# Half-block products for the forgetting heads' gates, and weight sums by adding transfers

## The chip, the cores and the metric

The kernel runs on one core of one Trainium2 chip, in one launch. The metric is the device time of an execution in microseconds (us), as the median of several runs. TensorE (PE) multiplies into PSUM; VectorE (DVE) and ScalarE (ACT) do elementwise work; GpSimd (POOL) and SyncE (SP) here mostly issue transfers, which run on the core's sixteen DMA engines. SP's transfers appear as queue q1 of the profile, POOL's as q0. Only POOL's transfers can add into what already lies at their destination.

## The reference

A decoder layer with two groups of eight heads: latent attention (MLA) and forgetting attention (FoX). Both groups have a gate path. The parts that this document needs:

```python
h = _rms_norm(x, g_pre)                     # x: 512 tokens x 2048, float32
proj = h @ w_in
(q_lat, kv_lat, k_rope_raw, gate_mla,
 fq, fk, fv, f_logit, gate_fox) = jnp.split(proj, split_points, axis=-1)
...
log_f = jax.nn.log_sigmoid(f_logit + b_forget)
c = jnp.cumsum(log_f, axis=1)               # per forgetting head
logits = q @ k * scale + c_query - c_key    # causal softmax, times v
...
o_fox = _fox_branch(fq, fk, fv, f_logit, b_forget) * jax.nn.silu(gate_fox)
o = jnp.concatenate([o_mla, o_fox], axis=-1) @ w_out
return x + _rms_norm(o, g_post)
```

`fv` and `gate_fox` are each a product of 512 x 2048 with 2048 x 1024. All arithmetic is float32.

## The kernel before

**Matrix products.** A float32 product is made from two parts of each operand: `hi`, a cast by Scalar (line 279 for weights), and `lo`, the remainder, subtracted by Vector (line 282). Three matmuls (lines 150 to 152) add hi x hi, hi x lo and lo x hi. Normalised x, without its row factor, lies on chip as `hh` and `hl`, sixteen tiles of 128 features x 512 tokens; the row factor is applied to the results (`rcol` by token as a column, `rrow` as a row).

**Chunks.** All weights pass as a list of chunks of at most 128 x 1024 numbers (512 KB). `load` lets SP bring a chunk to a `raw` tile four chunks ahead, `divide` splits it two chunks ahead of its matmuls. A chunk that is a sum of two blocks can be loaded as `raw` and `second` and joined by Vector (line 269).

**Two forms of a projection.** `proj_T` (used by `fox_q`, `fox_k`, `fox_g`) takes weights as the stationary operand and all 512 tokens as the moving one: 16 k-tiles x 2 heads x 3 matmuls of 512 columns for two heads. `product` makes one of the seven half-block products of a Strassen-Winograd scheme: x is cut into two halves of tokens and two halves of features, the weights into two halves of rows and two of columns, and p1, p2, p4, q6, g7, g5 and g3 replace eight half-size products. Each takes eight k-tiles in four chunks. With `turned=False` tokens end up on partitions, 48 matmuls of 512 columns a product; with `turned=True` features end up on partitions, 96 matmuls of 256 columns. Before the change the values of the forgetting heads ("v"), the latents ("l", turned) and the MLA gates ("m") are made like this; the gates of the forgetting heads are made by `fox_g`, two heads at a time, in four passes.

**Sums of x blocks.** `x_steps` puts x together again, `away_steps` makes the sums and sends them to DRAM, `fetches` bring them back and `divisions` split them.

**Sums of weight blocks.** `sum_blocks` lists background steps `bg`: SP copies one block to a DRAM tile (line 324), POOL adds the second (line 320). `paced` advances them by a step each `pace` k-tiles, twice that for the double-size steps of the output projection. A tiny mark written from the current weight tile (line 326) holds a step's copy to its place. The pace starts at 4; `set_pace` sets 20 after the first gates, 8 before the first queries, 12 before product q6 and 4.9 for the heads.

**Order.** After the first projection (`proj_first`, in which the order on Vector, Scalar and TensorE is fixed by hand) come: gates 0, p1, gates 1, p2, gates 2, g5, queries 0, g3, keys 0, q6, p4, g7, then the head pairs, with queries and keys of the next pair around the attention of the last; gates 3 come after the last keys. Elsewhere a planner orders each engine's instructions and may draw work forward. Small tasks in `todo` are taken one at a time after a k-tile (`pump`), or all at once (`drain`): the forget sums `fs` (17 steps on eight rows of 512), the rotary tables `rot`, the sums of x.

The values, scaled by `rcol`, are sent to DRAM (`v_out`) and brought back for each pair of heads. The finished gates wait on chip in `gf` tiles.

Of the kernel before, what the change touches and what calls it, by code (L numbers as in the profile page):

```python
# [66 lines left out]
def tile_hybrid_layer(  # L67
# [69 lines left out]
    def split_into(hi, lo, src, scale=None, pin=False):  # L137
        if scale is None:
            a = act.copy(hi, src)
            b = dve.tensor_tensor(out=lo, in0=src, in1=hi.bitcast(F32), op=ALU.subtract)  # L140
            if pin:
                in_order(a, b)
        else:
            act.mul(hi, src, scale)
            dve.scalar_tensor_tensor(
                out=lo, in0=src, scalar=scale, in1=hi.bitcast(F32), op0=ALU.mult, op1=ALU.subtract
            )

# [70 lines left out]
    raws, ready, up_chunks, early = {}, {}, set(), set()  # L219

    more, deep, seconds = [], [], [vr, 2]
    needs = {}

    def raw_tile(i):
# [4 lines left out]
        if i <= prods["g7", "v"][-1] and i % 5 < 2:  # L229
            return vr.tile([P, 1024], F32, tag="raw", name=f"raw{i}", bufs=2)  # L230
# [3 lines left out]
    def load(i, small=None):  # L234

        w, cols, k, n, width = chunks[i]
        assert state["step"] >= needs.get(i, -3) + 2
        if cols is None:
# [5 lines left out]
            if k is not None:  # L244
                if seconds and i not in early:
                    pool, bufs = seconds
                    second = pool.tile([P, 2, 512], F32, tag="second", name=f"second{i}", bufs=bufs)
# [24 lines left out]
    def divide(i):  # L272
# [10 lines left out]
        ready[i] = [t[:, :m].rearrange("p (k c) -> p k c", k=n) for t in (hi, lo)]  # L283

# [80 lines left out]
    AT = {"v": O_FV, "l": 0, "m": O_GM}  # L365
# [6 lines left out]
    for g in "vlm":  # L372
# [17 lines left out]
    for n in ("g0", "p1", "g1", "p2", "g2", "s5", "q0", "s3", "k0", "s6", "p4", "s7",  # L390
              "q1", "k1", "q2", "k2", "q3", "k3", "g3"):
        name = {"p1": "p1", "p2": "p2", "p4": "p4", "s5": "g5", "s3": "g3", "s6": "q6", "s7": "g7"}.get(n)
        if name:
            add_products([(name, "v")], plain_in)
            if n == "s5":
                early.update(prods["g5", "v"][2:])
        else:
            at = {"q": O_FQ, "k": O_FK, "g": O_GF}[n[0]] + 256 * (3 - int(n[1]))
            fox[int(n[1])][n[0]] = add_chunks(w_in, [(0, at, 256)], NK, 4, 256)
    add_products(  # L400
        [
            ("p1", "l"), ("p1", "m"), ("p2", "l"), ("p4", "l"), ("p2", "m"), ("p4", "m"),
# [188 lines left out]
    def proj_first(rng, banks):  # L591

        squares = deque(range(2 * NK))
# [232 lines left out]
    def rotary_tables():  # L826
        ifc = cst.tile([P, 2], F32, name="ifc")
        nc.sync.dma_start(ifc, inv_freq)
        pi = vr.tile([P, S], I32, tag="c", name="pos")
# [4 lines left out]
        def names():  # L834
            nonlocal n1, n2
            nn = vr.tile([P, 2, S], F32, tag="c", name="nn")
# [231 lines left out]
    def fox_q(p):  # L1068

        qb = [proj_bank(f"fq{p}{i}") for i in range(2)]  # L1070
        proj_T(fox[p]["q"], [(qb[i], P, two[i]) for i in range(2)], hh, hl)
        q = []
        wholes = slot(f"fw{p}")
        for i in range(2):
            t = tmp(f"fqt{p}{i}")
            dve.scalar_tensor_tensor(out=t, in0=qb[i], scalar=SC_F, in1=rrow, op0=ALU.mult, op1=ALU.mult)
            q.append(split(t, f"fq{p}{i}", first=P))
            whole_block(wholes, i, t)
# [26 lines left out]
    def values_into(tiles, cols, parts, pin=False):  # L1105
        for t in range(NT - 1):
            hi, lo = tiles[t]
            split_into(hi[:, cols], lo[:, cols], parts[t], pin=pin)
        last = act.copy(tiles[NT - 1][:, cols], parts[NT - 1])
        if pin:  # L1110
            in_order(last)
# [35 lines left out]
    hcol, ncol, rneg = (cst.tile([P, NT], F32, name=n) for n in ("hcol", "ncol", "rneg"))  # L1147
# [20 lines left out]
    def split_v(pair, both):  # L1168

        tiles = v_pair(f"fv{pair}")  # L1170
        return lambda: values_into(tiles, slice(0, 256), [both[:, t, :] for t in range(NT)], True)

    gates, gate_slots = {}, {}

    def fox_g(p, gb):

        proj_T(fox[p]["g"], [(gb[i], P, two[i]) for i in range(2)], hh, hl)
        if p == 3:
            drain()
        both = gate_slots[p] = slot(f"gf{p}")  # L1180
        for i in range(2):
            h = 2 * (3 - p) + i
            gates[h] = gate_of(gb[i], both[:, i, :], f"f{h}")
# [3 lines left out]
    def v_block(name):  # L1187
        return vr.tile([P, 2, S], F32, tag="c", name=name)
# [16 lines left out]
    act.mul(rneg, rcol, -1.0)  # L1205
# [11 lines left out]
    fox_g(0, [att_bank("fg00"), bank("pv", "fg01", 1)])  # L1217
    drain()
    set_pace(20)
    rot = rotary_tables()  # L1220
    wait(1)
    todo.extend([*fs[13:], *rot[:3]])
    A = two_of(proj_bank, "va")
    product("p1", "v", x_block(0, 0), A, True, True)
    drain()
    pa, pb = v_block("vpa"), v_block("vpb")
    scaled_copy(pa, A, 0, rcol)
    scaled_copy(pb, A, 2, rcol)
    todo.extend([*x_steps(0), *x_steps(1)])
    fox_g(1, two_of(proj_bank, "fg1"))  # L1230
    drain()
    todo.extend(rot[3:10])
    product("p2", "v", x_block(1, 0), A, False, True)
    drain()
    c11 = v_block("vc11")
    scaled_copy(c11, A, 0, rcol)
    v_out(c11, 0, 0)
    todo.extend([*x_steps(2), *x_steps(3)])
    fox_g(2, two_of(proj_bank, "fg2"))
    drain()  # L1240
    f3, f6, f7 = (fetches(n, "m") for n in ("g3", "q6", "g7"))
    d3, d6, d7 = (divisions(n, "m") for n in ("g3", "q6", "g7"))
    G = two_of(att_bank, "vg")
    product("g5", "v", operand("g5", "m"), G, True, True)
    c22 = v_block("vc22")
    scaled(c22, G, 2, pb, ALU.subtract, rcol)
    todo.extend([*f3, *rot[10:14], *d3, *rot[14:]])
    set_pace(8)
    q, wholes = fox_q(0)
    drain()  # L1250
    product("g3", "v", operand("g3", "m"), G, False, True)
    c12 = v_block("vc12")
    scaled(c12, G, 0, pa, ALU.subtract, rcol)
    todo.extend([*f6, *[lambda: None] * 3, *d6])
    k = fox_k(0, wholes)
    drain()
    set_pace(12)
    C = two_of(proj_bank, "vc")
    product("q6", "v", operand("q6", "m"), C, True, True)
    scaled(c12, C, 0, c12, col=rcol)  # L1260
    v_out(c12, 0, 1)
    todo.extend([*f7, *d7[:2]])
    B = two_of(proj_bank, "vp4")
    product("p4", "v", x_block(1, 2), B, True, True)
    drain()
    c21 = v_block("vc21")
    scaled(c21, B, 2, pb, col=rcol)
    product("g7", "v", operand("g7", "m"), C, False, True, side=d7[2:])
    c22, c22_sum = slot("vo22"), c22
    scaled(c22, C, 2, c22_sum, col=rcol)  # L1270
    v_out(c22, 1, 1)
    c21, c21_sum = slot("vo21"), c21
    scaled(c21, C, 2, c21_sum, col=rneg)
# [605 lines left out]
```

## Time and profile before

| what | us |
|---|---|
| median of 3 runs | 893.63 |
| lowest and highest run | 893.61, 893.68 |
| the profiled execution: span from first to last instruction | 892.3 |
| TensorE busy in it | 880.3 |
| VectorE, ScalarE, GpSimd busy | 660.2, 462.1, 72.8 |

The profile is of one execution, and gives its time as the span; the median is 1.3 us above that. Busy time of TensorE is a union of overlapping matmuls; the durations of single ones include the pipeline, so rates are read from starts. The DMA share is the mean busy share of the sixteen engines, summed over their queues. Values' and gates' products, first queries and first keys lie between 41.7 and 231 us, the pairs of forgetting heads between 231 and 418 us.

### The profile page before, as it was taken

The page shows a single profiled execution, that of the slowest core. Times are in us where ns is not written, and L with a number is a line of the kernel's source. Part 1 is how long each engine was busy: PE and PEld are TensorE (multiplying, and loading weights), DVE is VectorE, ACT ScalarE, POOL GpSimd, SP SyncE. Part 2 cuts the span into 40 slices and gives each one's busy share as a digit, 9 for nine tenths or more (in the row PEclk, how much of TensorE's full clock was granted, in tenths as well). Part 3 has the DMA queues.
Part 4 walks back from the last instruction along what each step waited for, and adds up shares of the span by engine and source line. Part 5 has one row for each costly group of instructions (what it writes and reads, how often), then busy time and mean ns, then how long its engine had stood idle before and what let it go on. Part 6 is the DMA issues. An engine that isn't in the chain of part 4 may idle for free.

```text
span 892.3 us, 12700 instructions
## 1 busy us (share of the span) xinstructions
PE 880.3 (99%) x4486; PEld 748.2 (84%) x4486; DVE 660.2 (74%) x1106; ACT 462.1 (52%) x841; POOL 72.8 (8%) x92
## 2 busy tenths in 40 slices
PE   9999999999999999999999999999999999999996
PEld 9988887888888888888998999788888888888885
DVE  4579995648665546477678999979787895988786
ACT  6944434334343433335455565657465776646383
POOL 0110110011110211010000000000000000000021
PEclk9999999999999999999999999999999999999999
DMA  9998798889999999997799885697988637799878
GB/s 319 277 265 241 212 341 279 250 214 315 261 282 275 238 230 225 247 231 186 243 412 410 329 303 178 167 275 166 221 182 215 153 111 233 228 323 322 264 214 254
DMA packets 139235, 225.07 MB, mean 252 GB/s; under 512 B 16898, under 2 KB 68892, under 8 KB 138148
## 3 DMA queue, kind: packets, MB, share of 16 engines
q1 hardware_dynamic: 124660, 184.19, 63.5%
q0 software_dynamic: 13776, 39.85, 22.2%
q8 instruction: 35, 0.57, 0.2%
q10 hardware_dynamic: 736, 0.22, 0.1%
q14 instruction: 28, 0.23, 0.1%
HBM read 209.53 MB, written 69.22 MB: 312 GB/s over the span
## 4 chain that ended last, share of the span: by engine, by line
PE 91%; DVE 4%; DMA 2%; ACT 2%; issue 1%; DVEq 0%; ACTq 0%; SPq 0%
PE fq L150 3%; PE fk L150 3%; PE fk L152 3%; PE fk L151 3%; PE fq L152 3%; PE fq L151 3%; PE fg L150 3%; PE in L614 3%; PE fg L151 3%; PE fg L152 3%; PE sm L657 3%; PE mq L152 2%; PE mq L150 2%; PE mq L151 2%; PE oa L150 2%; PE oa L152 2%
## 5 line engine op out<-in xcount | busy, mean ns | idle before, releaser
L282 DVE TENSOR_TENSOR wlo<-raw,whi 128x1024 fp32r<-128x1024 f32 (+3 forms) x220 | 261.0, 1189 | 134.0 <-ACT whi L279 125.8
L279 ACT CAST whi<-raw 128x1024 fp32r<-128x1024 f32 (+3 forms) x220 | 224.3, 1023 | 233.5 <-PE fk L151 31.8
L150 PE MATMUL fk<-h,whi 128*128 128x512 f32 x128 | 52.6, 411 | 0.0
L150 PE MATMUL fq<-h,whi 128*128 128x512 f32 x128 | 50.9, 397 | 0.0
L150 PE MATMUL fg<-h,whi 128*128 128x512 f32 x128 | 50.3, 393 | 0.0
L152 PE MATMUL fk<-h,wlo 128*128 128x512 f32 x128 | 50.2, 392 | 0.0
L151 PE MATMUL fk<-h,whi 128*128 128x512 f32 x128 | 50.2, 392 | 0.0
L152 PE MATMUL fq<-h,wlo 128*128 128x512 f32 x128 | 50.0, 391 | 0.0
L151 PE MATMUL fq<-h,whi 128*128 128x512 f32 x128 | 49.9, 390 | 0.0
L152 PE MATMUL fg<-h,wlo 128*128 128x512 f32 x128 | 49.9, 390 | 0.0
L151 PE MATMUL fg<-h,whi 128*128 128x512 f32 x128 | 49.9, 390 | 0.0
L675 ACT ACTIVATE pf<-pf,stf 128x128 f32<-128x128 f32 (+3 forms) x32 | 18.0, 562 | 61.4 <-DVE stf L666 61.4
L269 DVE TENSOR_TENSOR raw<-raw,second 128x1024 f32<-128x1024 f32 x32 | 39.0, 1219 | 0.5 <-DMA second<-in_w_out_dram 0.5
L614 PE MATMUL in<-whi,h 128*128 128x328 f32 x128 | 30.0, 321 | 0.0
L150 PE MATMUL mq<-ln,whi 128*128 128x512 f32 x72 | 29.2, 406 | 0.0
L152 PEld LDWEIGHTS fk<-h,wlo 128*128 128x128 f32 x128 | 24.1, 188 | 5.5
L152 PEld LDWEIGHTS fq<-h,wlo 128*128 128x128 f32 x128 | 24.0, 188 | 5.3
L152 PEld LDWEIGHTS fg<-h,wlo 128*128 128x128 f32 x128 | 24.0, 188 | 5.2
L151 PE MATMUL mq<-ln,whi 128*128 128x512 f32 x72 | 28.3, 393 | 0.0
L152 PE MATMUL mq<-ln,wlo 128*128 128x512 f32 x72 | 28.2, 392 | 0.0
L151 PEld LDWEIGHTS fg<-h,whi 128*128 128x128 f32 x128 | 24.1, 188 | 4.7
L150 PEld LDWEIGHTS fg<-h,whi 128*128 128x128 f32 x128 | 24.1, 188 | 4.7
(610 smaller groups left out, 2417.5 us busy)
## 6 DMA issues: line engine op xcount, KB each, us to landing
raw<-in_w_in_dram SPq DMA_DIRECT2D x96, 512.0 KB
raw<-in_w_out_dram SPq DMA_DIRECT2D x32, 512.0 KB
second<-in_w_in_dram SPq DMA_DIRECT2D x24, 512.0 KB
bmg<-awaymg SPq DMA_DIRECT2D x20, 256.0 KB
awaymg<-rmg POOLq DMA_DIRECT2D x8, 512.0 KB, 6.8
raw<-t6v SPq DMA_DIRECT2D x8, 512.0 KB
t7o<-in_w_out_dram SPq DMA_DIRECT2D x4, 1024.0 KB
t7o<-in_w_out_dram POOLq DMA_DIRECT2D x4, 1024.0 KB, 10.6
```

Source lines behind the costliest of these rows:

```text
L150: pe.matmul(o, ah, bh, start=first, stop=False, **kw)
L151: pe.matmul(o, ah, bl, start=False, stop=False, **kw)
L152: pe.matmul(o, al, bh, start=False, stop=last, **kw)
L269: tc.keep_in_program_order(dve.tensor_tensor(out=raw, in0=raw, in1=second, op=ALU.add))
L279: cast = act.copy(hi[:, :m], raw[:, :m])
L282: dve.tensor_tensor(out=lo[:, :m], in0=raw[:, :m], in1=hi[:, :m].bitcast(F32), op=ALU.subtract)
L614: pe.matmul(banks[t][:, :n], a[k][:, tss[t]], b[:, j, :], start=k == 0 and m == 0, stop=k == NK - 1 and m == 2,)
L657: pe.matmul(s[:, :nn], a[:, qs], c[:, :nn], start=(i == 0), stop=(i == len(pairs) - 1))
L675: act.activation(p, p, AF.Exp, bias=st[:, 0:1], scale=unit, accum_out=st[:, 1:2])
```

## The change

The gates of the forgetting heads become a fourth family, "g", of turned half-block products. Each of the seven products is made for the values and then for the gates, before anything of the forgetting heads but the first queries; the four `fox_g` passes go. The gate function (`gate_step`) is applied in place, two heads before each head pair.

The weight sums of "v" and "g" are no longer made in DRAM. p1's blocks are loaded into eight raw places (three of the common pool, five of `vr`) that stay. When a place has been split, `divide` issues the transfer to its next content: a POOL add of another block (g5, g7, q6, p4) or a plain SP load over it (g3). p2's blocks go through ordinary slots.

The sums of the products are kept unscaled; the values' row factor comes in when they are split for the heads (`split_v`). The rotary tables' steps, but for the sines, move into the first projection. The forget sums run steps 0 to 12 in the first pass, then step 0 again and steps 1 to 16 again. `set_pace(20)`, `(8)` and `(12)` are gone. The latents' part is put into another order (p2 of the latents before the pool of the heads is closed, p4 after p2 of the MLA gates), with the rotary key and the last heads' values now beside p1 and p2.

```diff
+        if cols in ("add", "over"):
+            return
+        if cols == "new":
+            at = vr if k >= 3 else wp
+            raws[i] = at.tile([P, 1024], F32, tag="raw", name=f"raw{i}", bufs=5 if at is vr else 3)
+            nc.sync.dma_start(raws[i].rearrange("p (k c) -> p k c", k=2), w)
+            return
...
         ready[i] = [t[:, :m].rearrange("p (k c) -> p k c", k=n) for t in (hi, lo)]
+        if i in follow:
+            j = follow[i]
+            raws[j] = raw
+            to = raw.rearrange("p (k c) -> p k c", k=2)
+            if chunks[j][1] == "add":
+                pool.dma_start(to, chunks[j][0], accum_op=ALU.add)
+            else:
+                nc.sync.dma_start(to, chunks[j][0])
...
-    for g in "vlm":
+    for g in "lm":
         sum_blocks(g, lambda j, h, c, g=g: in_block(g, j, h, c), ("t4", "t5"))
...
+    def in_place(name, h, c, how):
+
+        for g in "vg":
+            prods[name, g] = range(len(chunks), len(chunks) + 4)
+            for j in range(4):
+                i = len(chunks)
+                if how is None:
+                    up_chunks.add(i)
+                elif how == "new":
+                    last[g, j] = i
+                else:
+                    follow[last[g, j]] = i
+                    last[g, j] = i
+                chunks.append((in_block(g, j, h, c), how, "vg".index(g) * 4 + j if how == "new" else None, 2, 512))
...
+    add_fox(0, "q")
+    for name, h, c, how in (
+        ("p1", 0, 0, "new"), ("p2", 1, 0, None), ("g5", 0, 1, "add"), ("g3", 1, 1, "over"),
+        ("g7", 0, 1, "add"), ("q6", 0, 0, "add"), ("p4", 1, 0, "add"),
+    ):
+        in_place(name, h, c, how)
...
-    def proj_first(rng, banks):
-
+    def proj_first(rng, banks, beside):
+
+        beside = deque(beside)
...
+                for _ in range(2 if k > 4 else 0):
+                    if beside:
+                        beside.popleft()()
...
+    def gate_step(h):
+
+        g = gate_slots[h // 2][:, h % 2, :]
+        gate_of(g, g, f"f{h}")
...
+    rot = rotary_tables()
     with tc.manual_schedule(engines={mybir.EngineType.Activation, mybir.EngineType.DVE, mybir.EngineType.PE}):
-        proj_first(first, vb)
+        proj_first(first, vb, rot[:-1])
...
     todo.extend(fs[:13])
-    fox_g(0, [att_bank("fg00"), bank("pv", "fg01", 1)])
+    todo.append(fs[0])
+    todo.extend([*x_steps(0), *x_steps(1)])
+    q0 = fox_q(0, [att_bank("fq00"), bank("pv", "fq01", 1)], v_block)
     drain()
-    set_pace(20)
...
+    both_products("p1", (0, 0), False, A)
+    place(*P1)
+    put(*P1, A, None)
     drain()
+    todo.extend(fs[1:])
+    both_products("p2", (1, 0), False, A, False, side=((), f3))
...
+    G = banks("c")
+    both_products("g5", None, True, G, side=(d3, f7))
...
+    both_products("g3", None, True, G, False, side=(d7, f6))
...
+    both_products("g7", None, True, C, side=(d6, ()))
+    put(1, 0, C, "less")
+    both_products("q6", None, True, C, False)
...
+    product("p4", "v", x_block(1, 2), B["v"], True, True)
+    put(0, 1, {"v": B["v"]}, ALU.add)
+    v_out(to.pop(("v", 0, 1)), 1, 0)
+    product("p4", "g", x_wide(1, 2), B["g"], True, True, turned=True)
+    put(0, 1, {"g": B["g"]}, ALU.add)
     drain()
...
     set_pace(4.9)
+    wait(4)
+    todo.extend(lambda h=h: gate_step(h) for h in (6, 7))
     k = fox_k(0, wholes)
     drain()
...
-    fox_g(3, two_of(proj_bank, "fg3"))
-    o_of.extend(gate_slots[p] for p in (3, 2, 1, 0))
-    enqueue_values(heads)
+    o_of.extend(gate_slots)
```

More of the change, by code (lines that the diff above doesn't have):

```diff
@@ L244, in load @@
             if k is not None:
[L245 to L247 removed]
+                if seconds:
+                    at, bufs = seconds
+                    second = at.tile([P, 2, 512], F32, tag="second", name=f"second{i}", bufs=bufs)
                 else:
@@ new lines, in tile_hybrid_layer, with both_products, place @@
+    to = {}
+    def both_products(name, tokens, sums, o, first=True, side=((), ())):
+        for g, more in zip("vg", side):
+            wide = g == "g"
+            if sums:
+                parts = sums_wide(name) if wide else operand(name, "m")
+            else:
+                parts = (x_wide if wide else x_block)(*tokens)
+            product(name, g, parts, o[g], first, True, turned=wide, side=more)
+    def place(c, half):
+        to["v", c, half] = a = v_block(f"vc{c}{half}")
+        if c not in to:
+            to[c] = [slot(f"gf{2 * c + t}") for t in range(2)]
+        to["g", c, half] = [b[:, :, half * HALF : (half + 1) * HALF] for b in to[c]]
@@ new lines, in fold, with view, target, put @@
+    def fold(a):
+        return a.rearrange("p (f c) -> p f c", f=2)
+    def view(g, a):
+        return fold(a) if g == "g" else a
+    def target(g, c, half, t):
+        return to[g, c, half][t] if g == "g" else to[g, c, half][:, t, :]
+    def put(c, half, o, op, base=None):
+        for g in o:
+            for t in range(2):
+                out = target(g, c, half, t)
+                add = target(g, *base, t) if base else out
+                if op is None:
+                    act.copy(out, view(g, o[g][t]))
+                elif op == "less":
+                    dve.tensor_tensor(out=out, in0=add, in1=view(g, o[g][t]), op=ALU.subtract)
+                else:
+                    dve.tensor_tensor(out=out, in0=view(g, o[g][t]), in1=add, op=op)
```

251 lines of the change are left out of this document (109 added, 142 removed).

## The prediction

> **What bounds the kernel now.** I read the page of the profile first: span, TensorE's share, the DMA rows.
>
> ```profile
> span 892.3 us, 12700 instructions
> ...
> PE 880.3 (99%) x4486; PEld 748.2 (84%) x4486; DVE 660.2 (74%) x1106; ACT 462.1 (52%) x841; POOL 72.8 (8%) x92
> ...
> DMA  9998798889999999997799885697988637799878
> GB/s 319 277 265 241 212 341 279 250 214 315 261 282 275 238 230 225 247 231 186 243 412 410 329 303 178 167 275 166 221 182 215 153 111 233 228 323 322 264 214 254
> ...
> q1 hardware_dynamic: 124660, 184.19, 63.5%
> q0 software_dynamic: 13776, 39.85, 22.2%
> ```
>
> TensorE is busy 880.3 of 892.3 us, so what leaves it leaves the time, as long as nothing makes it wait. The DMA engines are the next resource: 63.5 + 22.2% of all sixteen. q1 is SP's queue (loads and copies), q0 POOL's (adds and writes back to DRAM).
>
> Second, TensorE's waits, to see where its feeding is already thin.
>
> ```profile
> PE mix L1724 <- ACT scaler L1723: 2.2, 1, 2.2
> ...
> PE vg L150 <- ACT whi L279: 0.9, 1, 0.9
> PE gdm L151 <- DVE wlo L282: 0.8, 1, 0.8
> PE vg L151 <- DVE wlo L282: 0.8, 1, 0.8
> ```
>
> The part that the diff rewrites has one stall: 0.9 + 0.8 = 1.7 us in the values' product g5 (vg). Third, the stages: first projection from its fifth k-tile on, gates and values, forgetting heads, and a stretch near the end that I need for a price (columns: busy us and counts, granted clock, DMA share, GB/s).
>
> ```profile
> core 0: us, PE busy (x) PEld busy (x) DVE busy (x) ACT busy (x) POOL busy (x), PEclk, DMA share, GB/s
> 18.40:41.70 23.30, 23.30 (x168) 23.23 (x166) 12.65 (x21) 21.17 (x65) 3.20 (x3) 1.00 1.05 294
> 41.70:231.00 189.30, 187.53 (x825) 153.90 (x825) 143.12 (x191) 80.15 (x107) 20.42 (x25) 1.00 0.89 263
> 231.00:418.00 187.00, 187.00 (x894) 155.65 (x893) 109.73 (x261) 72.48 (x159) 27.20 (x29) 1.00 0.96 248
> 868.70:882.00 13.30, 13.30 (x60) 11.04 (x59) 9.19 (x19) 6.68 (x13) 1.92 (x3) 1.00 1.09 264
> ```
>
> Vector has 46 us of air in the second stage and Scalar 109; the DMA engines are at 0.89 there and at 0.96 in the third. The share is summed over queues and overlaps a little: 1.09 is the highest of these rows, and I take it as what the engines can give.
>
> **The change, part by part.**
>
> *TensorE.* Four gate passes go; seven half-block products of the same 256-wide form as the latents' come.
>
> ```profile
> 54.37 0.39 PE L150 MATMUL fg<-h,whi 128*128 128x512 f32 x1
> ...
> 56.41 0.39 PE L150 MATMUL fg<-h,whi 128*128 128x512 f32 x1
> ```
> ```profile
> 494.76 0.28 PE L150 MATMUL gcl<-bmq,whi 128*128 128x256 f32 x1
> ...
> 502.92 0.28 PE L152 MATMUL gcl<-bmq,wlo 128*128 128x256 f32 x1
> ```
> ```profile
> L150 PE MATMUL fg<-h,whi 128*128 128x512 f32 x128 | 50.3, 393 | 0.0
> ```
>
> Starts tell the rate, since durations overlap. 54.37 to 56.41 is nine matmuls, 0.227 us each; 494.76 to 502.92 is 68, 0.120 each. Gates now: three groups (lines 150 to 152) of 128, 384 x 0.227 = 87.0 us. Afterwards 7 x 8 k-tiles x 4 x 3 = 672 x 0.120 = 80.6. **TensorE saves 6.4 us**, less than the eighth that seven products for eight promise, because two narrow matmuls (0.240) cost more than a wide one. The values' products keep number and width (48 x 0.227 = 10.9 us each).
>
> *Forget sums.* The new list runs its first step again and then steps 1 to 12 again: four more transposes on TensorE.
>
> ```profile
> 47.76 0.60 PE L766 MATMUL rf<-ident,rft 128*72 128x128 f32 x4
> 48.11 0.48 PE L150 MATMUL fg<-h,whi 128*128 128x512 f32 x1
> ```
>
> 48.11 - 47.76 = 0.35, with the turn-round +0.4 us. The repeated Vector steps (the reciprocal below is the longest) lie in Vector's 46 us of air.
>
> *Rotary tables* move into the first projection, where the order of Vector and Scalar is fixed by hand.
>
> ```profile
> L855 DVE SCALAR_TENSOR_TENSOR pos<-nn,pos 128x512 f32<-128x512 f32 x15 | 10.3, 689 | 0.2
> L798 DVE RECIPROCAL fd<-fd 8x512 f32<-8x512 f32 x1 | 3.3, 3345 | 0.0
> L847 DVE TENSOR_SCALAR nn<-pos 128x512 f32<-128x512 f32 x3 | 1.3, 424 | 0.0
> L848 DVE TENSOR_SCALAR nn<-nn 128x512 f32<-128x512 f32 x3 | 1.3, 423 | 0.0
> ```
>
> 10.3 + 1.3 + 1.3 and about 0.9 for the two first steps is 13.8 us on top of 12.65, 26.4 in a stretch of 23.3: 3.1 over. The x tiles are turned three k-tiles ahead and neighbouring Vector instructions overlap a little, so I take +1 us, bounds 0 and +3.
>
> *Vector and Scalar in the gates-and-values stage* get 16 more weight splits and the sums of the gates, and lose the joins and the early gate functions; a net of some ten us on Vector's 143 of 189. Nothing here, unless the DMA paces it all.
>
> *The transfers* decide. Three things happen in the same stretch, from 41.7 us to the last gate product. First, 32 of the 56 weight chunks (g5, g7, q6, p4, for values and gates, four each) become 512 KB adds from POOL into the raw place, issued when the chunk's former content has been split. Second, the pace lines (20, 8, 12) between forget sums and heads go, so the background sums keep the starting pace: one step (a copy by SP, then an add by POOL) every four k-tiles. The stretch has 16 + 14 x 8 = 128 k-tiles, 32 steps' worth: all sums of latents and MLA gates (16) and the small ones (4), then five or six of the double-size, half-pace ones, most of which stood in later stages before. Third, loads, write-backs and fetches as before. Prices of a 512 KB piece (0.524 MB), as time of all sixteen engines:
>
> Plain loads and copies, from the page: 184.19 MB in 0.635 x 892.3 = 567 us, 325 GB/s, **1.61 us**.
>
> Adds in DRAM, from the heads' stage (231 to 418), where they are most of q0:
>
> ```profile
> q0 software_dynamic: 5392, 14.42, 41.3%
> ...
> t7m<-in_w_in_dram POOLq DMA_DIRECT2D x4, 512.0 KB, 10.6
> ```
>
> 14.42 MB in 0.413 x 187 = 77.2 us, 187 GB/s, **2.81 us**.
>
> Adds into SBUF, the form of the new ones, stand only near the end, 868.7 to 882, where x is added into the finished rows:
>
> ```profile
> q0 software_dynamic: 946, 1.71, 70.3%
> q1 hardware_dynamic: 974, 1.78, 38.5%
> ...
> c<-in_x_dram POOLq DMA_DIRECT2D x3, 256.0 KB, 10.9
> ```
>
> 1.71 MB in 0.703 x 13.3 = 9.35 us, 183 GB/s, **2.87 us**, with q1 at 348 GB/s beside it. Both ends: not below a plain load, 1.61; not above the small-row adds between 330 and 340 us:
>
> ```profile
> q0 software_dynamic: 1025, 0.51, 43.7%
> ```
>
> 0.51 MB in 4.37 us, 4.5 for one piece. I take 2.87: same direction, same 2 KB rows.
>
> Writes to DRAM: q0 from 42 to 130 us, a mix of adds and such writes:
>
> ```profile
> q0 software_dynamic: 2596, 8.01, 35.0%
> ```
>
> 8.01 MB in 30.8 us, 2.0 us a piece; I take that for writes too.
>
> The Trainium skill puts it otherwise: the page "DMA: Bandwidth & Descriptors", section "Anatomy of one DMA — SWDGE (gpsimd) path", gives the moving part of a POOL transfer as bytes over 436 GB/s, which makes 1.2 us of a piece, add or not, as an estimate from that page. The same page's rules for kernel authors say that an accumulate reads its destination and writes it later. The tail's 183 GB/s speaks for the second sentence; what the first would make of the time is the second rival.
>
> Work until the last gate chunk has landed: plain, 24 loads + 2 of the next stage + 12 half-size fetches (6) + 28 copies = 60 x 1.61 = 97; adds into SBUF 32 x 2.87 = 92; adds in DRAM, 26 x 2.81 = 73 (small ones halved, some run earlier); writes 12 x 2.0 = 24. Together **286 us of work; at 1.09 it lasts 262 us**, to 41.7 + 262 = 304. Splitting and multiplying the last chunks adds about 8: 312. TensorE alone would get there at 41.7 + 21.8 + 7 x 10.9 + 80.6 = 220. **The DMA engines make it some 90 us late.** In a single pair of products: eight adds (23) and four steps (4 x 4.4 = 18) are 41 us for 22.4 of matmuls. It can't be made up: the heads' stage loses background sums, but TensorE was at 187.00 of 187.00 there. Late next is then everything from the first forgetting keys on, by the same amount.
>
> POOL's queue is in order, so a background add that waits for its copy holds the chunk adds behind it; SP's copies wait for their marks and hold loads. That is inside the 90 if the engines are full, and a few us more if not.
>
> **Sum** against the profiled span: 892.3 - 6.4 - 1.7 (the stall's place is swallowed) + 0.4 + 1 + 90 = 975.6. The median of the runs, 893.63, is 1.3 above that span, so **977 us**.
>
> **Rivals.**
>
> *Adds at the price of loads.* With 1.61 for the SBUF adds the work is 246, 225 us at 1.09; 41.7 + 225 + 8 = 275, 55 late: 942. For it: rows of 2 KB, like loads. Against: 183 beside 348 GB/s in the same 13 us.
>
> *The shares overprice and the engines keep up: faster.* To be hidden, the work must fit (220 - 8 - 41.7) x 1.09 = 186 us, not 286; a packet's time would have to contain a third of waiting that more traffic fills. For it: 412 GB/s in two slices at the digit 9, while other slices at 9 move 225. Against: those slices are plain loads, and no row above goes beyond 1.09. By the skill's 1.2 us the 130 pieces would be 156, and fit. Time: 892.3 - 6.4 - 1.7 + 0.4 + 1 + 1.3 = 887.
>
> *The background steps slide out of the stretch*, because the planner issues them late or the marks hold them. Without them: 32 plain (51.5) + 92 + 24 = 168, inside 186, but a pair with eight adds, 23 and a few fetches, just reaches 24: stalls of 2 to 15 us at the pairs, 889 to 902. Against it: before, the steps followed the pace.
>
> **How the numbers follow.** Forecast 0.60, loads' price 0.13, faster 0.17, slid steps 0.10. A difference under 0.2% (1.8 us) can't be told from none. Faster: nearly all of 0.17 and a little of the last, 0.18; same 0.04; slower 0.78. The forecast's own range is 942 (adds at the price of loads) to 1005 (SBUF adds half-way to 4.5: 3.7 each, 312 of work, 116 late); the slower cases reach down to 889, and half of the faster one lies above 886. Range 886 to 1005: half of the faster case and the top of mine, some 0.16, are outside.
>
> **What would show it.** Right: in the stages g5 to p4 the DMA share stands at 1.0 to 1.1 with q0 well over half of it; TensorE waits for casts and subtractions that wait for a transfer into a raw place; pairs last 40 us or more instead of 22.4; narrow gate matmuls still start 0.120 apart inside a chunk; the heads' stage is full. The rotary step shows as TensorE waiting for Vector before 42 us. Wrong: a share below 0.95 there with TensorE full, or a stall that ends on Vector with the raw long landed.

## The result, and the profile after

The changed kernel takes 993.1 us (median of 4 runs, 992.0 to 995.8) against 893.65 of the kernel before, a ratio of 1.111 (95% interval 1.1085 to 1.1135): 99 us slower. The forecast was 977, its own range 942 to 1005.

From the page of the profile after (span, engines, then TensorE, its clock and the DMA engines in 40 slices of 24.8 us):

```profile
span 990.5 us, 13300 instructions
...
PE 909.3 (92%) x4778; PEld 777.0 (78%) x4778; DVE 682.3 (69%) x1137; ACT 479.2 (48%) x858; POOL 104.7 (11%) x117
...
PE   9896589878768899999999989999999999999997
...
PEclk9999689888889999999999999999999999999999
DMA  9999999999999999953445999834332325779878
```

The span grew by 98.2 us. TensorE's idle time went from 12.0 to 81.2 us, and its busy time rose by 29.0 although it has less to do. The low digits of TensorE lie in slices 4 to 14 (74 to 347 us), and there the DMA engines stand at 9 without a break. They stay at 9 up to 421 us; after that, in the rest of the heads' stage, they have time to spare (5, 3, 4, 4, 5), which they did not have before. Work was drawn forward into a stretch that could not hold it.

The stretch by products, in the trace after (columns: busy us and counts of the engines, granted clock, DMA share, GB/s). p1 and p2 lie between 70.5 and 150, g5 and g3 from there to 203, g7 and q6 to 275, p4 to 312:

```profile
core 0: us, PE busy (x) PEld busy (x) DVE busy (x) ACT busy (x) POOL busy (x), PEclk, DMA share, GB/s
47.40:70.50 23.10, 23.10 (x107) 19.02 (x107) 20.98 (x42) 13.91 (x25) 6.28 (x7) 1.00 1.01 267
70.50:93.00 22.50, 17.94 (x103) 15.26 (x100) 19.25 (x28) 8.27 (x10) 11.36 (x12) 1.00 1.08 236
93.00:119.00 26.00, 10.26 (x49) 9.16 (x50) 11.87 (x17) 3.58 (x5) 5.73 (x6) 0.67 1.09 285
119.00:150.00 31.00, 26.57 (x139) 22.09 (x139) 23.78 (x25) 14.28 (x17) 4.71 (x6) 0.84 0.92 270
...
176.80:203.00 26.20, 25.64 (x144) 22.52 (x145) 17.32 (x19) 11.26 (x13) 12.75 (x12) 0.87 1.06 222
203.00:234.50 31.50, 25.04 (x146) 21.82 (x145) 13.26 (x16) 10.13 (x14) 14.05 (x13) 0.89 1.13 241
234.50:274.70 40.20, 27.46 (x147) 23.62 (x145) 13.58 (x17) 8.78 (x9) 11.77 (x12) 0.87 1.09 247
274.70:312.00 37.30, 28.89 (x144) 24.30 (x144) 16.98 (x20) 10.64 (x11) 5.10 (x6) 0.86 1.06 247
```

And the queues between 47.4 and 312 us:

```profile
q0 software_dynamic: 15974, 37.20, 70.7%
q1 hardware_dynamic: 17472, 30.69, 34.3%
```

The DMA share is at 0.92 to 1.13 in every stage, two thirds of it POOL's queue (70.7 of 105%). What TensorE waits for, the three largest:

```profile
PE va L150 <- ACT whi L284: 12.2, 2, 11.9
PE gd L150 <- ACT whi L284: 10.4, 2, 5.2
PE ga L152 <- DVE wlo L287: 7.9, 2, 6.2
```

These are the splits of the values' and gates' weights, and Scalar itself waits for transfers: its casts stood idle 118.4 us behind loads and adds into raw places.

```profile
L284 ACT CAST whi<-raw 128x1024 fp32r<-128x1024 f32 (+3 forms) x232 | 236.4, 1023 | 327.7 <-DMA raw<-in_w_in_dram 118.4
```

Three landmarks: the first queries, which end the first projection (after), the first forgetting keys (after), and the first MLA queries, in the kernel before and after.

```profile
47.38 0.40 PE L150 MATMUL fq<-h,whi 128*128 128x512 f32 x1
...
312.23 0.50 PE L150 MATMUL fk<-h,whi 128*128 128x512 f32 x1 [1.02 <-ACT whi L284]
...
685.09 0.39 PE L150 MATMUL mq<-ln,whi 128*128 128x512 f32 x1
```
```profile
587.07 0.39 PE L150 MATMUL mq<-ln,whi 128*128 128x512 f32 x1
```

From the MLA queries to the end nothing differs (305.4 us after, 305.2 before). Of the 98.0 us that they come later, 5.7 are lost in the first projection (47.4 against 41.7), 86.1 between 47.4 and 312.2 (264.9 us, where TensorE alone would need the prediction's 21.8 + 7 x 10.9 + 80.6 = 178.7), and 14 in the heads and latents; 6.4 + 1.7 - 0.4 are won.

### The profile page after: what moved, and what is told of

Its sections match the earlier page's. It is cut to its first block, busy times and chain, and to the rows that moved or that the text cites. A ratio compares the mean times of both kernels' runs of the same rounds, so it can differ in the third digit from the quotient of the medians.

```text
span 990.5 us, 13300 instructions
## 1 busy us (share of the span) xinstructions
PE 909.3 (92%) x4778; PEld 777.0 (78%) x4778; DVE 682.3 (69%) x1137; ACT 479.2 (48%) x858; POOL 104.7 (11%) x117
## 4 chain that ended last, share of the span: by engine, by line
PE 53%; DMA 5%; DVE 4%; issue 1%; ACT 1%; DVEq 0%; SPq 0%; ACTq 0%
PE sm L695 2%; PE fq L150 2%; PE fq L152 2%; PE fq L151 2%; DMA raw<-in_w_in_dram 2%; DMA second<-in_w_in_dram 2%; PE fk L150 2%; PE fk L151 2%; PE fk L152 2%; PE mq L152 2%; PE mq L150 2%; PE mq L151 2%; PE sf L695 2%; PE oa L152 1%; PE oa L150 1%; PE oa L151 1%
## 5 line engine op out<-in xcount | busy, mean ns | idle before, releaser
L287 DVE TENSOR_TENSOR wlo<-raw,whi 128x1024 fp32r<-128x1024 f32 (+3 forms) x232 | 275.4, 1191 | 205.7 <-ACT whi L284 203.7
L284 ACT CAST whi<-raw 128x1024 fp32r<-128x1024 f32 (+3 forms) x232 | 236.4, 1023 | 327.7 <-DMA raw<-in_w_in_dram 118.4
L1772 POOL DMA_DIRECT2D c<-in_x_dram x8 | 7.0, 987 | 380.6 <-ACT c L1771 380.6
L294 POOL DMA_DIRECT2D raw<-in_w_in_dram x32 | 45.5, 1828 | 4.4 <-DMA raw<-in_w_in_dram 3.4
L274 DVE TENSOR_TENSOR raw<-raw,second 128x1024 f32<-128x1024 f32 x24 | 29.3, 1220 | 5.2 <-DMA second<-in_w_in_dram 5.0
L150 PEld LDWEIGHTS fk<-h,whi 128*128 128x128 f32 x128 | 24.1, 188 | 5.5 <-ACT whi L284 1.2
L151 PEld LDWEIGHTS fq<-h,whi 128*128 128x128 f32 x128 | 24.4, 190 | 4.5
L150 PEld LDWEIGHTS fq<-h,whi 128*128 128x128 f32 x128 | 24.4, 190 | 4.4
L151 PEld LDWEIGHTS fk<-h,whi 128*128 128x128 f32 x128 | 24.1, 189 | 3.9
```

Source lines behind the costliest of these rows:

```text
L150: pe.matmul(o, ah, bh, start=first, stop=False, **kw)
L151: pe.matmul(o, ah, bl, start=False, stop=False, **kw)
L274: tc.keep_in_program_order(dve.tensor_tensor(out=raw, in0=raw, in1=second, op=ALU.add))
L284: cast = act.copy(hi[:, :m], raw[:, :m])
L287: dve.tensor_tensor(out=lo[:, :m], in0=raw[:, :m], in1=hi[:, :m].bitcast(F32), op=ALU.subtract)
L294: pool.dma_start(to, chunks[j][0], accum_op=ALU.add)
```

## Experiments

The theory after the result was the prediction's: the engines cannot move the adds and the drawn-forward steps in time. Its rivals were the order of the queues, and later Vector.

**e1: the slow pace back.**

```diff
     q0 = fox_q(0, [att_bank("fq00"), bank("pv", "fq01", 1)], v_block)
     drain()
+    set_pace(20)
```

> The changed kernel with one line more: pace 20 for the background sums from the first product on, as the kernel before had it. Theory (the transfer engines' work decides): some 24 of the 30 background steps leave the stretch, 24 x (1.61 + 2.81) = 106 us of work; 286 - 106 = 180, at 1.09 it lasts 165 us, less than the 179 of matmuls, so only a few us at single pairs stay: 905 to 920 us in place of 993. Rival (the chain of adds into one raw place, 18.6 us from issue to landing, and POOL's queue are too slow by themselves): at most 20 us are won, 970 or more.

927.5 us, ratio 1.0367 (1.0337 to 1.0398): 66 of the 99 us are gone. The theory holds in its direction, but the time is 7.5 us above the expected range. In its trace g5 and g3, and g7 and q6, run without a wait:

```profile
140.93 0.40 PE L150 MATMUL vc<-whi,smg 128*128 128x512 f32 x1
...
185.77 0.40 PE L150 MATMUL vd<-whi,bmg 128*128 128x512 f32 x1
```

44.84 us for two pairs is 22.4 a pair, exactly the 10.9 + 11.5 that the prediction took, so TensorE's saving of 6.4 us is real. But p1 and p2 take 70.7 us (70.26 to 140.93) for 44.8 of work. Two readings of e1's trace point to two causes: SP's queue waits 37 us in one place for a transfer of POOL's queue, and Vector is full from 47 to 93 us:

```profile
SPq L247 <- DMA awaymg<-rmg: 51.5, 4, 37.0
```
```profile
47.00:70.50 23.50, 23.50 (x110) 19.42 (x109) 20.93 (x42) 13.94 (x23) 6.13 (x7) 1.00 1.02 264
70.50:93.00 22.50, 18.67 (x109) 15.98 (x108) 22.37 (x33) 8.41 (x11) 9.65 (x11) 1.00 1.05 208
```

p2's weights are loaded into places that held the sums of x (`rmg`), so SP waits until POOL has sent those to DRAM, and POOL until Vector has made them.

**e2: the 32 chunk adds as plain loads of the same queue.**

```diff
             if chunks[j][1] == "add":
-                pool.dma_start(to, chunks[j][0], accum_op=ALU.add)
+                pool.dma_start(to, chunks[j][0])
```

> The changed kernel with the 32 transfers into the raw places as plain POOL loads in place of adds (it leaves out the weights' sums, so its products are not the layer's). Same queue, same order, same waits. Theory: only the price of the add goes, 32 x (2.87 - 1.61) = 40 us of engine work, 37 at 1.09: 993 - 37 = 956, bounds 945 to 970. Rival (POOL's queue in order, a background add that waits for its copy holding the chunks behind it): nothing is won, 985 to 995.

961.1 us, ratio 1.0745 (1.0718 to 1.0772), inside the theory's bounds. The same 37.2 MB of q0, between 47 and 285 us of e2:

```profile
q0 software_dynamic: 11888, 37.23, 59.1%
q1 hardware_dynamic: 17686, 31.59, 39.1%
```

q0's time is 0.591 x 238 = 140.7 us against 0.707 x 264.6 = 187.1 with the adds: 46.4 us for 32 adds, 1.45 us of all engines for each, over a plain load. The prediction had 2.87 - 1.61 = 1.26.

**e3: the first loads of the raw places held in program order on SP.**

```diff
-            nc.sync.dma_start(raws[i].rearrange("p (k c) -> p k c", k=2), w)
+            tc.keep_in_program_order(nc.sync.dma_start(raws[i].rearrange("p (k c) -> p k c", k=2), w))
```

> The changed kernel with the eight first loads into the raw places held in program order on SP's queue; the order on all other engines is the same. In the changed kernel five of them are issued between 16 and 23 us, ahead of the first projection's own weights, and TensorE ends that projection 5.7 us later than before. Theory: those five loads (5 x 1.61 = 8 us of the engines) are the cause: the projection ends near 42 us again, and the total falls by 0 to 5.7, since the engines have the same work to do later. Rival (the rotary steps on Vector): the projection still ends near 47 us.

999.65 us, and the first projection still ends at 46.8 us. The theory of the run fell: other copies moved up in the place of p1's loads. The 6.5 us more than the changed kernel are there when the keys start (318.2 against 312.2); why was not followed up.

**e4: the kernel before, without its three pace lines.**

```diff
-    set_pace(20)
...
-    set_pace(8)
...
-    set_pace(12)
```

> The kernel before without its three lines that set pace 20, 8 and 12, so that the background sums keep pace 4 up to the heads; nothing else is changed. Theory: about 18 more background steps fall between 41.7 and 231 us, 18 x 4.4 = 79 us of work on top of 0.89 x 189 = 168; 247 at 1.09 is 227, 38 over the 189: 920 to 935 us in place of 893.6. Rival (the pace does not matter, the adds into the raw places alone do): within 5 us of 893.6.

939.0 us, ratio 1.0503 (1.0471 to 1.0535), 4 us above the expected range. The lost pace alone costs 45 us in a kernel that has none of the new adds, and it shows in the same kind of wait:

```profile
PE vp L150 <- ACT whi L279: 15.9, 1, 15.9
PE vg L150 <- ACT whi L279: 10.0, 2, 8.5
```

**e5: e1 with the forget sums' steps once**, and **e6: no background step before g5, then the pace 20.** They set Vector (A) against the queues (B) as the cause of the slow p1 and p2 in e1.

```diff
-    todo.extend(fs[:13])
     todo.append(fs[0])
...
     drain()
+    set_pace(20)
```
```diff
+    set_pace(1000)
     q0 = fox_q(0, [att_bank("fq00"), bank("pv", "fq01", 1)], v_block)
...
+    set_pace(20)
     both_products("g5", None, True, G, side=(d3, f7))
```

(The first extract is e5, with the pace line of e1; the second is e6.)

> The slow pace of e1 (927.5 us), and the forget sums' steps only once: steps 0 to 12 no longer run in the first pass, so Vector gets about 9.5 us less between 47 and 93 us (where e1 shows it busy 20.93 of 23.5 and 22.37 of 22.5). e1 loses some 26 us in p1 and p2 (70.8 to 140.8 us for 44.8 us of matmuls). Theory A: Vector is full, so the sums of x are late, so are the transfers that take them to DRAM, and p2's weight loads, which wait for the places of those sums, come late; then 918 to 922. Theory B: the queues block each other (SP's load waits for a transfer of POOL, which stands behind a background add that waits for a copy of SP); then 925 to 929. My prediction's +0.4 us for the repetition agrees with B.

> No background step at all until g5, then one every 20 k-tiles (e1: every 4 during the first queries, then every 20). Theory B of the run before (SP and POOL wait for each other through the background steps): p1 and p2 together take 46 to 52 us instead of 70.8, and the time falls from 927.5 to 905 to 912. Theory A (Vector is full between 47 and 93 us): the step's two transfers are not the cause, and the time is 922 to 928.

e5: 921.9 us, ratio 1.0315 (1.0278 to 1.0353). e6: 925.1, ratio 1.0345 (1.0321 to 1.0369). p1 and p2 take 62.2 us in e5 (69.67 to 131.82) and 66.2 in e6 (71.21 to 137.40), 70.7 in e1. B as it was put (46 to 52 us) falls, and both times lie where A put them; but A's run wins 8.5 of the 26 us and B's 4.5, so neither explains the loss alone. The intervals of the two ratios overlap, and the times themselves do not rank them. The repetition that the prediction put at +0.4 us, with Vector's steps covered, costs 5.6 us at the slow pace by the medians (e5's runs take 918 to 926 us, e1's 925 to 929; the intervals just touch, and e5's trace is of its fastest run).

**e7: the changed kernel with the rotary steps in p2.**

```diff
-        proj_first(first, vb, rot[:-1])
+        proj_first(first, vb, ())
...
-    todo.extend([*x_steps(2), rot[-1], *x_steps(3)])
+    todo.extend([*x_steps(2), *x_steps(3)])
...
-    todo.extend(fs[1:])
+    todo.extend(rot)
     both_products("p2", (1, 0), False, A, False, side=((), f3))
+    drain()
+    todo.extend(fs[1:])
```

> The changed kernel with one part moved: the rotary tables' steps run in p2 and not in the first projection; nothing else differs. If Vector, full from 28 us on, stretches the first projection, it ends at 42 to 43 us instead of 47.4, and the time is 985 to 991 (993.1 with the steps in the projection), as the transfers that set the pace afterwards start earlier by as much. If the loads that come late in the projection stretch it, it still ends at 46 to 47.5, and the time is 992 to 995.

994.3 us, and the first projection ends at 48.6, later if anything. The second theory for the 5.7 us fell too. What was left is a line of the diff that stands in no extract above: besides the new places of p1, `raw_tile` lost two places that the first projection's chunks used.

```diff
-        if i <= prods["g7", "v"][-1] and i % 5 < 2:
-            return vr.tile([P, 1024], F32, tag="raw", name=f"raw{i}", bufs=2)
```

SP's issues show it, before (line 259) and after (line 264):

```profile
9.74 1.89 SPq L259 DMA_DIRECT2D raw<-in_w_in_dram  x2
...
12.20 1.56 SPq L259 DMA_DIRECT2D raw<-in_w_in_dram  x2
```
```profile
7.44 2.61 SPq L264 DMA_DIRECT2D raw<-in_w_in_dram  x2
...
19.93 1.81 SPq L264 DMA_DIRECT2D raw<-in_w_in_dram  x2
```

Before, the loads go on to 13.8 us; after, they stop at 10.0 and go on only when a place is free, at 19.9. TensorE then stands, in the kernel after:

```profile
28.45 0.42 PE L649 MATMUL in<-whi,h 128*128 128x328 f32 x1 [2.07 <-ACT whi L284]
```

**e8: e6, e5 and e7 together** (no step before g5, sums once, rotary steps in p2).

> The three edits together: no background step before g5 and one every 20 k-tiles from there, forget sums once, rotary steps in p2. If the three losses that I name (p1 and p2 some 26 us, the first projection 5, Vector's repeated steps up to 9 of the 26) are all there is before the heads, the time is 893 to 903, and what stays above the kernel before (893.8) lies after the heads, in the latents (about 5 us in e1). If the adds themselves still can't be hidden in these products, 905 to 920.

910.4 us, ratio 1.0182 (1.0166 to 1.0199). p1 and p2 now take 46.5 us (70.72 to 117.19), against 70.7 in e1 and 44.8 of work: 24 of the 26 us are won back, where the forget sums alone won 8.5 (e5) and the background steps alone 4.5 (e6). It takes Vector and the queues together; what the rotary steps' move adds by itself at the slow pace was not tried. The time still lies above the expected 893 to 903: the first projection still ends at 47.9 us, and a part of the loss moved on to g5 and g3, which take 52.7 us:

```profile
140.00:162.00 22.00, 18.50 (x107) 15.48 (x106) 20.30 (x23) 8.60 (x11) 8.44 (x7) 1.00 0.97 200
...
480.00:500.00 20.00, 14.78 (x90) 12.28 (x88) 17.34 (x22) 7.77 (x10) 1.60 (x3) 1.00 1.04 401
```
```profile
PE gc L150 <- DVE gf L1314: 3.0, 1, 3.0
```

g3 adds onto the banks of g5, so its gate matmuls wait until Vector has taken g5's result out, behind the forget steps. The second row, at 480 to 500 us, is the same loss that the changed kernel has at 560 to 600 (below).

**e9: five places for the first projection's chunks again.**

```diff
     def raw_tile(i):
...
+        if i in first and i % 5 < 2:
+            return vr.tile([P, 1024], F32, tag="raw", name=f"raw{i}", bufs=5)
```

> The changed kernel, with two of the first projection's places given back: of every five of its weight chunks two lie in the pool of p1's blocks (as before the change), so that five raw places serve it and not three. In the trace of before SP has issued the loads of all first eight chunks by 13.8 us, after the change it stops at 10.0 us and goes on at 19.9; Scalar's cast then waits 3.8 us for a transfer, TensorE 2.1 for the cast. If the places are the cause, that wait is gone and the first projection ends at 42 to 43 us (47.4 with three places, and 46.6 and 48.6 in e3 and e7, so neither loads drawn ahead nor the rotary steps set it); the time is 986 to 991, as the transfers that set the pace later start earlier. If they are not, it ends at 46 to 48.5, time 992 to 995.

993.6 us: the time is the same. The wait of 2.07 us is gone and the projection ends at 45.2 and not at 47.4; what remains is Vector, which is full (3.96 of 4 us), and TensorE now waits for its subtraction:

```profile
27.17 0.42 PE L651 MATMUL in<-wlo,h 128*128 128x328 f32 x1 [1.44 <-DVE wlo L289]
```
```profile
40.00:44.00 4.00, 3.58 (x24) 3.31 (x24) 3.96 (x8) 2.09 (x7) 0.00 (x0) 1.00 0.88 231
```

So the expectation of 42 to 43 us was wrong for one edit alone. The keys start at 310.6, still 1.6 us ahead of the changed kernel. The gain is lost behind them: TensorE stands 8.6 us at one place where it stands 3.5 in the changed kernel (below), because the cast ahead waits 15.5 us for its load, and the MLA queries start at 686.5 (685.1). That fits a time that the transfers set, but 2 us are also less than the spread of the runs (989.0 to 995.8).

**e10: e8 with the five places, the forget steps spread over g5 and g3** (one every second k-tile).

```diff
     drain()
-    todo.extend(fs[1:])
+    for s in fs[1:]:
+        todo.append(s)
+        wait(1)
     place(0, 0)
```

> e8 (910.4 us) with the five places of e9, and with the forget sums' steps spread over g5 and g3, one every second k-tile. e8 still loses 6 us in the first projection and about 6 between 117 and 162 us, where TensorE waits for Vector (wlo 2.2, gf 3.0) in g5 and g3. If both go: 897 to 902. If the places matter only once the transfers bind: 904 to 910.

```profile
41.82 0.39 PE L150 MATMUL fq<-h,whi 128*128 128x512 f32 x1
```

With both the places and the rotary steps out of it, the first projection ends at 41.8 us, as before the change. Five places against three, without rotary steps, are worth 6 to 7 us there (47.9 and 48.6 in e8 and e7), the rotary steps 3.3 (45.2 in e9, with five places). The whole took 908.45 us, ratio 1.0158 (1.014 to 1.0177), where 897 to 902 were expected: of 6.1 us won at the start, 2.4 are left at the keys (234.8 against 237.2). TensorE's wait for Vector's sums between g5 and g3 grew from 3.0 to 5.3 us, and the two pairs take 56.2 us (52.7 in e8): 7.3 idle and some 3.4 at a granted clock of 0.94. Spreading the steps did not help.

**e11: e10 with p4 of the latents ahead of p2 of the MLA gates**, as before the change.

```diff
-            ("p1", "l"), ("p1", "m"), ("p2", "l"), ("p2", "m"), ("p4", "l"), ("p4", "m"),
+            ("p1", "l"), ("p1", "m"), ("p2", "l"), ("p4", "l"), ("p2", "m"), ("p4", "m"),
```

(with the two `product` calls in that order, `side=f6` at the first and `along(d6, f5)` at the second)

> e10 with p4 of the latents ahead of p2 of the MLA gates again, as before the change (the two stand next to each other after the deep pool opens). In e8 TensorE loses 6.4 us between 480 and 510 us there, with the transfer engines at 1.04 and 400 GB/s; p4's sums need two loads a chunk, and two such products now follow each other. If their order is the cause, 3 to 5 us less than e10; if the later opening of the pool is, within 1 us of e10.

901.4 us, ratio 1.0082 (1.0067 to 1.0096), 7 less than e10. The stage itself accounts for the expected size: from 480 to 500 us TensorE is busy 19.04 us (15.04 in e10), with the transfers just as full. The other 3 us are not located; the two traces, of e10's fastest run and e11's slowest, differ by 2.3 us only, 5.4 won behind the keys and 3.1 lost ahead of them.

```profile
480.00:500.00 20.00, 19.04 (x84) 15.43 (x84) 17.73 (x20) 9.97 (x12) 1.06 (x2) 1.00 1.04 403
```

By an estimate, two products of sums in a row need 16 pieces, 16 x 1.61 = 25.8 us of the engines, in 22.4 us of matmuls; a plain product between them gives the loads time. The later opening of the pool, which stays, is not the cause of what was won. This is the fastest version of the change that was run, and it is still slower than the kernel before. What it loses lies mostly in g5 and g3 (56.0 us for 44.8 of work) and in the first queries (26.7 for 21.8), against the 6.4 us of fewer matmuls.

**e12: e11 with Vector's steps spread again**: 11 of the 20 rotary steps in the first projection, one a k-tile, the rest and half of the forget steps in p2, the others in g5.

```diff
-        proj_first(first, vb, ())
+        proj_first(first, vb, rot[:11])
...
-                for _ in range(2 if k > 4 else 0):
+                for _ in range(1 if k > 4 else 0):
...
-    todo.extend(rot)
+    todo.extend([*rot[11:], *fs[1:]])
     both_products("p2", (1, 0), False, A, False, side=((), f3))
-    drain()
-    for s in fs[1:]:
-        todo.append(s)
-        wait(1)
     place(0, 0)
```

> e11 (901.4 us) with Vector's small steps spread more evenly: 11 of the 20 rotary steps in the first projection, one a k-tile (e10 shows Vector busy 12.8 of 23.6 us there), the rest and half of the forget sums' steps in p2, the other half in g5. In e11 TensorE waits 5.4 us for the gates' sum of Vector behind g5 and about 2 for its splits in g5. If Vector's load in g5 is the cause, 894 to 898; if the waits only move to p1 and p2 (21.7 of 23 and 17.5 of 23 us busy in e11), 899 to 903. Faster than the kernel before (893.7) it is only if the 6.4 us of fewer matmuls outweigh all that is left.

910.1 us, ratio 1.0172 (1.0155 to 1.0189), a miss. The wait for g5's sums is gone, and g5 and g3 take 44.8 us, which is all work; but p1 and p2 are slow again (70.27 to 125.97, 55.7 us), with Vector at 23.00 of 23 us:

```profile
65.00:88.00 23.00, 23.00 (x130) 20.21 (x130) 23.00 (x33) 10.37 (x12) 10.80 (x12) 1.00 1.01 243
```

So the loss of 11 us only changed its place. That e12 is slower than e11 lies mostly in p4, which takes 29.0 us (215.7 to 244.7) against 22.4: between 212 and 246 us Scalar's casts wait 17.9 us for transfers into raw places, 4.1 in e11. Why those come later was not looked into. Whether any spread of Vector's work in this stage reaches 893 is open.

## Why the prediction was right, and where it was off

**Transfers until the last gate chunk: right, in its terms.** Forecast: q1 97 us of work, q0 92 + 73 + 24 = 189, at 1.09, so that the keys start at 312. Measured between 47.4 and 312: 0.343 x 264.6 = 90.8, 187.1, and 1.05; the keys start at 312.2. Smaller work and a smaller capacity nearly cancel (265 us against 262 + 8), and the stretch begins 5.7 us later: that the start of the keys agrees to 0.2 us is luck. The price of an add into SBUF, which was taken from 13 us at the end of the kernel before, has nearly held: e2 puts its surcharge at 1.45 us, not 1.26. By the rule of the Trainium skill ("DMA: Bandwidth & Descriptors", section "Anatomy of one DMA — SWDGE (gpsimd) path") a piece would move in 1.2 us, as an estimate from its figure, and the 130 pieces would fit if that held for both queues. The trace does not agree: q0 moved 37.20 MB in 187.1 us of all engines, 199 GB/s and 2.6 us a piece.

**The two causes: right, and each costs time.** The chunk adds and the drawn-forward steps were put into one sum. e1 takes the steps out of the stretch (-66 us), e2 the adding (-32), e4 puts the steps alone into the kernel before (+45). What e1 leaves, 34 us, is not the adds alone: e8 wins 17 of them with the adds in place.

**"It can't be made up; late next is everything after by the same amount": the step that failed.** The forecast's sum missed the profiled span by 14.9 us (975.6 against 990.5), and nearly all of that, 14 us, lies behind 312.2 us. The heads and latents lose time of their own (before the change TensorE stood 1.0 us in all between 231 and 587):

```profile
312.20:335.00 22.80, 22.24 (x97) 18.10 (x98) 8.90 (x9) 5.03 (x5) 3.30 (x4) 1.00 0.98 249
335.00:360.00 25.00, 21.50 (x92) 17.53 (x91) 14.28 (x40) 9.91 (x20) 2.01 (x2) 0.93 1.01 267
360.00:400.00 40.00, 38.79 (x188) 31.62 (x187) 22.97 (x48) 16.14 (x35) 1.97 (x2) 1.00 0.97 246
...
560.00:600.00 40.00, 34.21 (x221) 30.51 (x220) 33.90 (x39) 17.28 (x22) 2.16 (x4) 0.96 1.04 393
```

0.6 + 3.5 + 1.2 + 5.8 = 11.1 us idle (none from 400 to 560), and some 3 at a lower clock (7% of 25, 4% of 40). The first part is the backlog of transfers running into the heads. The 3.5 us show how; Scalar and TensorE in order of time:

```profile
340.88 1.04 ACT L284 CAST whi<-raw 128x1024 fp32r<-128x1024 f32 x1 [9.93 <-DMA raw<-in_w_in_dram]
...
342.35 0.29 ACT L127 COPY fw<-fkt 128x128 f32<-128x128 f32 x1
```
```profile
342.69 0.49 PE L695 MATMUL sf<-fw 128*128 128x128 f32 x2 [3.50 <-ACT fw L127]
```

The keys are long multiplied, but their copy stands behind a weight cast on Scalar, and that cast waits 9.9 us for its load. The second part, at 560 to 600, is the new order of the latents, a part of the diff that the prediction did not price at all; e11 undoes it and wins most of the loss there.

**First projection, +1 with bounds 0 and +3: off.** It cost 5.7. The rotary steps themselves are worth 3.3 us (e9 and e10), just over the upper bound; the two lost places, which the prediction did not see, are worth 6 to 7 without the rotary steps, and the two overlap. In the changed kernel that hardly shows in the time: e9 wins 2.2 us there, loses them again at a wait for a load behind the keys, and is not faster. That the transfers set the time there in any case is argued, not shown by a run.

**Forget sums, +0.4: off at the slow pace**, where e5 puts the repetition at 5.6 us. What it costs in the changed kernel itself, where the transfers bind, no run shows.

**TensorE saves 6.4 us: right** (44.84 us for two pairs in e1), and not to be seen in the busy time of the changed kernel, which the lower clock inflates.

**The marks.** The share (1.02 to 1.13 from g5 to p4, once above the 1.09 that was taken as the most the engines give) and q0 well over half were met, and so were the narrow matmuls 0.120 apart (86.00 to 88.52 us, 21 of them). Pairs of 40 us or more were not, on the whole: seven pairs take 242 us, 34.5 each, and from g5 to p4 only q6 reaches 40. In the first projection TensorE waited for Scalar (2.1 us) more than for Vector (0.5), which was the sign of the lost places; and the heads' stage was full of transfers only up to 421 us. The mark came from a pair with eight adds and four steps, while the prediction's own sum, 262 us less the first queries, gave 34.

**The rivals.** *Adds at the price of loads* would have been 942; e2, where they are loads, takes 961, so that case was also priced too low, by the same losses in the first projection and after the keys and some waits in p1 and p2. *The engines keep up* fell with q0's 187 us. *The steps slide out* did not happen, but e1 is that case, and 927.5 lies far above its 889 to 902: it counted TensorE, transfers and no Vector, whose 46 us of air were an average over 189 us. In the first 89 of them, in the kernel before, only 7.7 were free:

```profile
41.70:131.00 89.30, 89.30 (x395) 73.43 (x395) 81.63 (x124) 39.13 (x55) 12.74 (x17) 1.00 0.90 261
```

## What to carry to other kernels

Price an adding transfer by its time on the engines, not by its bytes, and count every background step that a changed pace draws into the same stretch: a pace line is work moved, here worth 45 to 66 us of time. Air on an engine is to be read stage by stage where small steps are moved: the rotary and forget steps were covered by the average of Vector's stage and not by the windows they landed in. And a diff that changes what a pool of buffers is used for takes places away from whoever used them first; look for the loads that now stop early.

## What the runs showed of the hardware

**The clock after a stall.** In the first projection of the changed kernel TensorE stood still from about 26.4 to 28.4 us; afterwards the granted clock fell to half for some three microseconds, and not at once (the clock is the third number from the end):

```profile
29.00:30.00 1.00, 0.67 (x4) 0.68 (x5) 1.00 (x3) 1.00 (x5) 0.00 (x0) 1.00 1.17 322
30.00:31.00 1.00, 1.00 (x6) 1.00 (x5) 0.96 (x2) 1.00 (x5) 0.00 (x0) 0.57 1.15 271
31.00:32.00 1.00, 1.00 (x5) 0.95 (x5) 1.00 (x3) 1.00 (x5) 0.00 (x0) 0.50 1.11 278
32.00:33.00 1.00, 1.00 (x7) 1.00 (x6) 0.97 (x2) 0.26 (x2) 0.94 (x1) 0.50 0.83 227
```

Most of the longer stalls are followed by the same, down to 0.67 over 93 to 119 us. That is why TensorE's busy time rose by 29.0 us while its work fell by 6.4: the mean granted clock fell from 0.998 to 0.961, and 0.039 x 990.5 less 0.002 x 892.3 is 37 us, near the 35.4 to be explained. The Trainium skill's page "TensorE: Matmul & The Clock Gate", Part 1, has the clock at half after an idle window of about 3.4 us and back after a busy one; the three microseconds agree, while a wait of 2.07 us, followed by one of 0.46 (in the trace, at 29.3), was enough here. Where the transfers set the time, the slow clock should only fill time in which TensorE would have waited; that is argued, not shown.

**What an add costs the engines.** While both queues were full, 257 GB/s were moved between 47.4 and 312 us with over half of the bytes in POOL's queue, against 393 to 403 GB/s at the same DMA share near the latents, where nearly all are loads (13 to 20% of the bytes in POOL's queue).
